# Filters' first transform stage as 32x32 block matmuls, and adaLN sums in pieces, in layer 0's MLP

## The chip, the cores and the metric

The kernel runs on one core of one Trainium2 chip. The metric is the device time of one execution in microseconds (us). The engines of a core work side by side, each through its own list of instructions in order, and wait for each other through semaphores: TensorE (matmuls; PE, its loads of weights PEld), VectorE (DVE), ScalarE (ACT), GpSimd (POOL) and SyncE (SP, which here only issues DMAs).

## What is computed

Two layers over 1024 tokens of width 1024. Layer 0 mixes with a recurrent block (RG-LRU), layer 1 with an order-2 Hyena operator; each is followed by a squared-ReLU MLP of hidden width 4096. Every sub-layer is normed and modulated by sums of the condition vector (adaLN). All data are fp32.

```python
for i in range(DEPTH):
    mod = (cond @ ada_w[i] + ada_b[i])[:, None, :]
    sh1, sc1, g1, sh2, sc2, g2 = jnp.split(mod, 6, axis=-1)
    u = modulate(x, norm_g[i, 0], sh1, sc1)
    ...
    x = x + g1 * y
    x = x + g2 * squared_relu_mlp(modulate(x, norm_g[i, 1], sh2, sc2), mlp_w1[i], mlp_w2[i])

def hyena_filters(L, ...):
    h = jnp.sin(...)                                   # three small layers
    h = (h @ fw4).reshape(L, N_DIRS, HYENA_ORDER, D_MODEL)
    h = h * jnp.exp(-t * deltas)[:, None, None, :]
    h = h / jnp.sum(jnp.abs(h), axis=(0, 1), keepdims=True)
    k = jnp.concatenate([fwd[:1] + bwd[:1], fwd[1:], zeros, jnp.flip(bwd[1:], 0)], axis=0)
    return jnp.fft.rfft(k, axis=0)
```

The filters don't depend on the tokens, so the kernel works them out beside layer 0's MLP, ahead of layer 1, which needs them.

## The kernel before

Activations lie with the 1024 features on 8 tiles of 128 partitions and the 1024 tokens on the columns, in two halves c of 512. A weight tile comes by DMA on SyncE's queue (`raw`, two buffers), ScalarE rounds it to `whi` and VectorE takes the rest, `wlo` (three buffers each), and a product is three matmuls: high by high, high by low, low by high (`mm3`, `gemm`, `gemm2`; lines 133 to 152). Each of these takes one pass through TensorE.

`mlp` goes through eight hidden blocks `fb` of 512. In each, the first matrix gives four hidden tiles for both halves (48 matmuls for a tile and its two halves); `use` squares the rectified values and splits them into `hh` and `hl`. The second matrix then gives the eight output tiles (24 matmuls each for both halves), and `upd` (line 745) adds them to the stream `xs` on VectorE. TensorE's results go to six PSUM banks in turn (`psum`), small sums to a bank of their own (`psum_st`).

From block 1 on, `hook` is called after each hidden tile (4 a block) and each output tile (8 a block), and runs one step of `filters`. There are 64 groups: 16 frequencies g by 4 quarters u. `head(i)` fetches features, lets ScalarE compute the decay into `ht`, multiplies features by weights with three one-pass matmuls, multiplies by the decay on VectorE (line 383) and sums absolute values. `tail(i - 2)` does the first stage of the Fourier transform of a group: one plain fp32 matmul of `ht` by `mf`, a 128x128 matrix with four equal 32x32 blocks on its diagonal; in the trace it is two passes (line 396). ScalarE copies the result to `fe` and a DMA writes it out. The last group of a quarter (g = 0) has another first block, and closes the norm.

`ada_half` computes half of one adaLN vector: eight times a DMA of 128x512 weights (`adaw`, two buffers, line 190) and a multiply-add on VectorE into `acc` (lines 193, 195), then four small fp32 matmuls with ones, eight passes in the trace (line 198), and a short addition. Fourteen halves are left at the MLP of layer 0: two are done inside block 0, then two at the end of each block, with all their instructions issued together.

The order of each engine's list comes from a scheduler that simulates the program; `tc.issue_after(x)` keeps instructions behind x in that order.

Of the kernel before, what the change touches and what calls it, by code (L numbers as in the profile page):

```python
# [16 lines left out]
P = 128  # L17
D = 1024
# [28 lines left out]
def tile_block(ctx: ExitStack, tc: tile.TileContext, a, out, dbg=None):  # L47
# [19 lines left out]
    def psum():  # L67
        return psp.tile([P, 512], F32, tag="ps", name=nm("ps"))
# [116 lines left out]
    def ada_half(pool, l, j, h):  # L185
# [12 lines left out]
            nc.tensor.matmul(ps[:, t:t + 1], acc[:, t * P:(t + 1) * P], ones[:, 0:1], start=True, stop=True)  # L198
        nc.vector.tensor_tensor(mod[:, l, j, 4 * h:4 * h + 4], ps[:, 0:4], vcols("ada_b", 48 * l + 8 * j + 4 * h, 4), op=ALU.add)


    def norm_stats(pool, xs, n, keep, aside=False):

# [82 lines left out]
    def filter_pos(fp, fb, aside):  # L286

        pos = fp.tile([66, 512], F32, tag="pos", name="pos")
        nc.sync.dma_start(pos, a["pos"])
        w1 = fp.tile([66, P], F32, tag="fw1", name="fw1")  # L290
        nc.sync.dma_start(w1, a["fw1"])
        w23 = fp.tile([P, 2, P], F32, tag="fw23", name="fw23")
        nc.sync.dma_start(w23, a["fw23"])
        h = pos
        MAGIC = 12582912.0
        C1 = 6.28125
        C2 = 0.0019350051879882812
        C3 = 2 * math.pi - C1 - C2
        LIM = 3.1415925
        for n in range(3):  # L300
            ps = psum()
            nc.tensor.matmul(ps, w1 if n == 0 else w23[:, n - 1], h, start=True, stop=True)
            s = fp.tile([P, 512], F32, tag="fs", name=nm("fs"), bufs=2)
            nc.vector.tensor_scalar(s, ps, vcol(f"hy_fb{n + 1}", 0), vcol("hy_freq", 0), op0=ALU.add, op1=ALU.mult)
            k = fp.tile([P, 512], F32, tag="fk", name=nm("fk"), bufs=2)
            nc.vector.tensor_scalar(k, s, 1.0 / (2 * math.pi), MAGIC, op0=ALU.mult, op1=ALU.add)
            nc.vector.tensor_scalar(k, k, MAGIC, None, op0=ALU.subtract)
            for cc in (C1, C2, C3):
                nc.vector.scalar_tensor_tensor(s, k, -cc, s, op0=ALU.mult, op1=ALU.add)
            nc.vector.tensor_scalar(s, s, LIM, -LIM, op0=ALU.min, op1=ALU.max)  # L310
            h = fp.tile([P, 512], F32, tag="fh", name=nm("fh"), bufs=2)
            nc.scalar.activation(h, s, AF.Sin)
            aside(n)
        tap("fh3", h)

        lo, up = h[0:64], h[64:128]
        hh = fp.tile([P, 1024], F32, tag="hh", name="hh")
        nc.sync.dma_start(hh[0:64, 512:1024], up)
        nc.sync.dma_start(hh[64:128, 0:511], lo[:, 1:512])
        nc.sync.dma_start(hh[64:128, 1023:1024], lo[:, 0:1])  # L320
        nc.scalar.copy(hh[0:64, 0:512], lo)
        nc.vector.tensor_copy(hh[64:128, 511:1023], up)
        hp = fp.tile([P, 16, 4, 32], F32, tag="hp", name="hp")
        nc.gpsimd.memset(hp, 0.0)
        for half in range(2):
            src = hh[64 * half:64 * half + 64]
            if half:
                src = src[:, ::-1]
            src = src.rearrange("p (t m j g) -> p g m j t", t=16, m=2, j=4, g=8)
            dst = hp.rearrange("p (g m) j t -> p g m j t", m=2)[64 * half:64 * half + 64]  # L330
            for m in range(2):
                for j in range(4):
                    eng = nc.scalar.copy if j % 2 else nc.vector.tensor_copy
                    eng(dst[:, :, m, j, 16 * half:16 * half + 16], src[:, :, m, j, :])
        for n, t in enumerate(split(fb, "hps", hp.rearrange("p g j t -> p (g j t)"), [P, 2048], 1, "v")):
            nc.sync.dma_start(hpd[:, :, n].rearrange("g p c -> p g c"), t.bitcast(F32).rearrange("p (g c) -> p g c", g=16))

# [5 lines left out]

    def filters(fp):

        LAG = 2
        st = {}
        steps = [(u, g) for u in (0, 2, 1, 3) for g in list(range(1, 16)) + [0]]
        mf = fp.tile([P, 2, P], F32, name="mf")
        nc.sync.dma_start(mf, a["mf"])  # L350
        tpos = fp.tile([P, 16], F32, name="tpos")
        nc.sync.dma_start(tpos, a["tpos"])
# [37 lines left out]
                nc.vector.tensor_tensor(acc, acc, ab, op=ALU.add)  # L390

        def tail(i):
            u, g = steps[i]
            o, c = u // 2, u % 2
            p2 = psum()
            nc.tensor.matmul(p2, mf[:, 1 if g == 0 else 0], st.pop(("ht", i)), start=True, stop=True)
            e = fp.tile([P, 512], F32, tag="fe", name=nm("fe"), bufs=2)
            nc.scalar.copy(e, p2)
            if g == 0:

                acc = st["acc", u]
                pc = psum_st()
                for t in range(4):
                    nc.tensor.matmul(pc[:, t:t + 1], acc[:, t * P:(t + 1) * P], ones[:, 0:1], start=True, stop=True)
                nc.vector.reciprocal(rn[:, o, 4 * c:4 * c + 4], pc[:, 0:4])
                pr = psum_rb()
                nc.tensor.matmul(pr, ones, acc, start=True, stop=True)
                sk = fp.tile([17, 512], F32, tag="sk", name=nm("sk"), bufs=1)
                nc.sync.dma_start(sk, a["skip"][:, o, c * 512:(c + 1) * 512])
                nc.vector.tensor_tensor(sk, pr[0:17, :], sk, op=ALU.mult)  # L410
                nc.vector.tensor_tensor(e[0:17, :], e[0:17, :], sk, op=ALU.add)
            b = prow(g)
            nc.sync.dma_start(fd[u][:, b:b + 29:4].rearrange("f k d -> k f d"), e)

        def step(i):
            if i < len(steps):
                head(i)
            if i >= LAG:
                tail(i - LAG)
        return [lambda i=i: step(i) for i in range(len(steps) + LAG)]  # L420

# [283 lines left out]
                use(m, c, pp[c])  # L705


    def mlp(load, l, xs, r0, ada_step, fin=None, normed=lambda: None, hook=lambda: None):

        with ExitStack() as st:  # L710
            uh, ul = [None, None], [None, None]
# [9 lines left out]
            for fb in range(8):  # L721
# [3 lines left out]
                def use(m, c, ps):  # L725
                    r = hp.tile([P, 512], F32, tag="r", name=nm("r"), bufs=2)
                    nc.scalar.activation(r, ps, AF.Relu)
                    h_ = hp.tile([P, 512], F32R, tag="hh", name=nm("hh"), bufs=8)
                    nc.scalar.activation(h_, r, AF.Square)
                    nc.vector.tensor_tensor(r, r, r, op=ALU.mult)  # L730
                    l_ = hp.tile([P, 512], F32R, tag="hl", name=nm("hl"), bufs=8)
                    nc.vector.tensor_tensor(l_, r, h_.bitcast(F32), op=ALU.subtract)
                    hh[c][m], hl[c][m] = h_, l_
                    if c == 1 and fb:
                        hook()

                in_gemm(load, lambda m: a["mlp_w1"][l, 4 * fb + m], 4, uh, ul, use, 3 if fb == 0 else 0)
                if fb == 0:
                    with tc.issue_after(applied[1].ins):
                        ada_step()  # L740
                        ada_step()

                def upd(m, c, ps, o=0, n=512):
                    cs = slice(c * 512 + o, c * 512 + o + n)
                    nc.vector.scalar_tensor_tensor(xs[m][:, cs], ps[:, :n], g2[:, m:m + 1], xs[m][:, cs], op0=ALU.mult, op1=ALU.add)  # L745

                def w2(q, mm, rnd):
                    pp = [psum() for c in rnd]
# [5 lines left out]
                for rnd in ((0,), (1,)) if fb == 7 else ((0, 1),):  # L754
                    for q in range(4):
# [3 lines left out]
                        for mm in range(2):  # L759
                            w2(q, mm, rnd)  # L760
                            if fb and rnd[0] == 0:
                                hook()
                            if fin and fb == 7:
                                fin[0](2 * q + mm, 512 * rnd[0], 512)
                                if rnd == (1,) and q == 0:
# [1 line left out]
                if fin and fb == 7:  # L767
# [8 lines left out]
                    fin[1](768, 256)  # L776
                    fin[2](512, 256)
                    fin[2](768, 256)
                ada_step()
                ada_step()  # L780

    def gemm2_n(pp, w, off, rh, rl, kt):
        if len(pp) == 2:
# [328 lines left out]
    def ada_step(pool):  # L1112
        if ada_todo:
            l, j, h = ada_todo.pop(0)
            ada_half(pool, l, j, h)
            if h == 1 and j == 4:
                make_scale(scl[:, 2 * l + 1], vcols("norm_g", 16 * l + 8, 8), mod[:, l, 4])
            if h == 1 and j == 1:
                make_scale(scl[:, 2], vcols("norm_g", 16, 8), mod[:, 1, 1])

    wst[0], load = open_w()
    wpool = wp_[0]
# [26 lines left out]
        tap("x1", xs[k], k)  # L1149
    with ExitStack() as st:  # L1150
        adap = st.enter_context(tc.tile_pool(name="adap", bufs=1, reuse_waits="tile"))
        ffst, todo = ExitStack(), []

        def normed():

            nst[0].close()
            todo.extend(filters(ffst.enter_context(tc.tile_pool(name="ff", bufs=1, side="right", reuse_waits="tile"))))

        def hook():
            if todo:  # L1160
                todo.pop(0)()
        mlp(load, 0, xs, r0, lambda: ada_step(adap), None, normed, hook)
        assert not ada_todo and not todo
        ffst.close()
    tap("rn", rn)
    open_n()
# [33 lines left out]
def _consts():  # L1200
# [47 lines left out]
    c1_, d1_ = coef(np.arange(32), 1.0), coef(np.arange(16), 2.0)  # L1248
    m1 = np.zeros((2, 16, 8, 4, 32))
    md = np.zeros((2, 4, 32, 16, 8))  # L1250
    mf = np.zeros((2, 4, 32, 4, 32))
    for j in range(4):
        for m in range(2):
            m1[m, :, 4 * m + j, j, :] = c1_[:16]
            md[m, j, :, :, 4 * m + j] = d1_.T
        mf[:, j, :, j, :] = c1_
    mf[1, 0, 16, 0, :] = c1_[0]

    def lay(m, w=P):
        m = m.reshape(-1, P, w).transpose(1, 0, 2)  # L1260
# [9 lines left out]
    pos2 = np.ascontiguousarray(np.concatenate([pos[:512].T, pos[512:].T], 0))  # L1270
    deltas = np.abs(np.linspace(math.log(1e-2) / 1.5, math.log(1e-2) / 0.3, D, dtype=f32))
    full = np.concatenate([t, t[back]], 0)
    tpos = np.ascontiguousarray(full.reshape(32, 2, 4, 8).transpose(3, 1, 2, 0).reshape(16, P).T)
    decay = np.ascontiguousarray(np.broadcast_to(-deltas, (P, D)))
    return dict(m1=lay(m1), md=lay(md), mf=lay(mf), m2=lay(m2[FORD], 192), mi=lay(mi[FORD]), pos=pos2, tpos=tpos, decay=decay)


def _layout(i):
# [81 lines left out]
```

## Time and profile before

| | |
|---|---|
| median of 3 runs | 2838.49 us (2838.48 to 2840.58) |
| profiled execution | 2838.23 us, span 2836.4 us |
| busy: TensorE matmuls | 2682.9 us, 95% |
| busy: loads of weights | 2046.7 us, 72% |
| busy: VectorE | 1524.7 us, 54% |
| busy: ScalarE | 1044.6 us, 37% |
| granted TensorE clock, mean | 0.972 |

Layer 0's MLP lies between about 560 and 1390 us of the span. A matmul's record begins when TensorE takes it up; its end is modelled, so neighbouring matmuls overlap in the record, and the pace is read from starts. `idle before` is time in which the engine stood still just ahead of an instruction, with what ended it.

### The profile page before, as it was taken

The page shows a single profiled execution, that of the slowest core. Times are in us where ns is not written, and L with a number is a line of the kernel's source. Part 1 is how long each engine was busy: PE and PEld are TensorE (multiplying, and loading weights), DVE is VectorE, ACT ScalarE, POOL GpSimd, SP SyncE. Part 2 cuts the span into 40 slices and gives each one's busy share as a digit, 9 for nine tenths or more (in the row PEclk, how much of TensorE's full clock was granted, in tenths as well). Part 3 has the DMA queues.
Part 4 walks back from the last instruction along what each step waited for, and adds up shares of the span by engine and source line. Part 5 has one row for each costly group of instructions (what it writes and reads, how often), then busy time and mean ns, then how long its engine had stood idle before and what let it go on. Part 6 is the DMA issues. An engine that isn't in the chain of part 4 may idle for free. (4 is left out here: it accounts for less than half of the span.)

```text
span 2836.4 us, 29311 instructions
## 1 busy us (share of the span) xinstructions
PE 2682.9 (95%) x11194; PEld 2046.7 (72%) x11194; DVE 1524.7 (54%) x2077; ACT 1044.6 (37%) x1566; POOL 256.7 (9%) x162
## 2 busy tenths in 40 slices
PE   6689898999999999999999999878899999999998
PEld 1577777788777777778888773333588888888887
DVE  7666665875455455443843347647475333333336
ACT  5457577552333333322632223323343211122213
POOL 0223333010000000000100013212000000000000
PEclk8789999999999999999999999999899999999999
DMA  8431123344344344331312325565331111111112
GB/s 302 123 119 45 45 75 104 111 136 138 108 132 138 106 128 138 92 92 47 126 56 93 104 98 154 149 161 167 126 89 45 52 46 52 45 53 45 52 45 97
DMA packets 120269, 286.33 MB, mean 101 GB/s; under 512 B 11770, under 2 KB 27900, under 8 KB 120002
## 3 DMA queue, kind: packets, MB, share of 16 engines
q1 hardware_dynamic: 109618, 261.40, 30.2%
q10 hardware_dynamic: 8256, 14.68, 1.8%
q0 software_dynamic: 2256, 8.39, 0.9%
q8 instruction: 88, 1.44, 0.2%
q14 instruction: 51, 0.42, 0.0%
HBM read 212.86 MB, written 37.75 MB: 88 GB/s over the span
## 5 line engine op out<-in xcount | busy, mean ns | idle before, releaser
L152 PE MATMUL ps<-u,whi 128*128 128x512 f32 x2696 | 734.3, 393 | 0.0
L113 ACT CAST whi<-raw 128x1024 fp32r<-128x1024 f32 x206 | 216.3, 1050 | 1107.6 <-PE ps L152 1012.7
L152 PEld LDWEIGHTS ps<-u,whi 128*128 128x128 f32 x2696 | 504.7, 188 | 113.9 <-issue 7.2
L115 DVE TENSOR_TENSOR wlo<-raw,whi 128x1024 fp32r<-128x1024 f32 x206 | 261.9, 1271 | 473.3 <-ACT whi L113 472.6
L152 PE MATMUL ps<-u,wlo 128*128 128x512 f32 x1348 | 418.5, 390 | 0.1
L152 PE MATMUL ps<-hh,whi 128*128 128x512 f32 x896 | 296.4, 409 | 0.0
L152 PEld LDWEIGHTS ps<-u,wlo 128*128 128x128 f32 x1348 | 252.9, 188 | 53.2 <-DVE wlo L115 0.7
L152 PE MATMUL ps<-hh,wlo 128*128 128x512 f32 x896 | 281.8, 390 | 0.0
L152 PE MATMUL ps<-hl,whi 128*128 128x512 f32 x896 | 280.3, 389 | 0.0
L152 PEld LDWEIGHTS ps<-hh,whi 128*128 128x128 f32 x896 | 168.2, 188 | 51.5 <-issue 17.3
L134 PE MATMUL ps<-u,whi 128*128 128x512 f32 (+1 forms) x508 | 195.3, 386 | 3.5 <-POOL u L260 2.9
L133 PE MATMUL ps<-u,whi 128*128 128x512 f32 (+1 forms) x508 | 187.2, 385 | 11.5 <-ACT u L259 11.5
L135 PE MATMUL ps<-u,wlo 128*128 128x512 f32 (+1 forms) x508 | 193.1, 382 | 1.8 <-DVE wlo L115 1.8
L152 PEld LDWEIGHTS ps<-hl,whi 128*128 128x128 f32 x896 | 168.2, 188 | 36.2 <-issue 1.0
L152 PEld LDWEIGHTS ps<-hh,wlo 128*128 128x128 f32 x896 | 168.1, 188 | 35.1
L745 DVE SCALAR_TENSOR_TENSOR big<-ps,mod,big 128x512 f32<-128x512 f32 (+1 forms) x132 | 91.6, 731 | 185.3 <-PE ps L152 177.7
L745 DVE SCALAR_TENSOR_TENSOR x<-ps,mod,x 128x512 f32<-128x512 f32 x128 | 91.3, 746 | 147.0 <-PE ps L152 139.0
L260 POOL TENSOR_TENSOR u<-nu,u 128x512 fp32r<-128x512 f32 x24 | 33.9, 1413 | 1010.6 <-ACT u L259 1001.4
L195 DVE SCALAR_TENSOR_TENSOR acc<-adaw,cond,acc 128x512 f32<-128x512 f32 x98 | 73.5, 750 | 92.1 <-DMA adaw<-in_ada_w_dram 90.7
L133 PEld LDWEIGHTS ps<-u,whi 128*128 128x128 f32 x508 | 98.0, 194 | 30.1 <-ACT u L259 12.2
L134 PEld LDWEIGHTS ps<-u,whi 128*128 128x128 f32 x508 | 98.2, 193 | 25.5 <-POOL u L260 5.9
L135 PEld LDWEIGHTS ps<-u,wlo 128*128 128x128 f32 x508 | 97.5, 192 | 20.2 <-DVE wlo L115 3.0
(223 smaller groups left out, 3821.3 us busy)
## 6 DMA issues: line engine op xcount, KB each, us to landing
raw<-in_mlp_w_dram SPq DMA_DIRECT2D x136, 512.0 KB
adaw<-in_ada_w_dram SPq DMA_DIRECT2D x112, 256.0 KB
fd<-fe SPq DMA_DIRECT2D x64, 256.0 KB
ft<-fd SPq DMA_DIRECT2D x64, 256.0 KB
e<-big SPq DMA_DIRECT2D x64, 256.0 KB
eraw<-in_ada_w_dram SPq DMA_DIRECT2D x24, 512.0 KB
raw<-in_hy_w_in_dram SPq DMA_DIRECT2D x24, 512.0 KB
big<-e ACTq DMA_DIRECT2D x48, 256.0 KB
```

Of the source, the lines that this page charges most:

```text
L113: lsplit[0] = nc.scalar.copy(hi, raw)
L115: lsplit[1] = nc.vector.tensor_tensor(lo, raw, hi.bitcast(F32), op=ALU.subtract)
L133: first = pin(nc.tensor.matmul(ps, wh, rh, start=start, stop=False))
L134: pin(nc.tensor.matmul(ps, wh, rl, start=False, stop=False))
L135: pin(nc.tensor.matmul(ps, wl, rh, start=False, stop=stop))
L152: nc.tensor.matmul(pp[c], x, y[c][k], start=first, stop=last)
L195: nc.vector.scalar_tensor_tensor(acc, w, s, acc, op0=ALU.mult, op1=ALU.add)
L260: applied[k % 2] = (nc.vector if k % 2 else nc.gpsimd).tensor_tensor(ul[k], u, uh[k].bitcast(F32), op=ALU.subtract)
L745: nc.vector.scalar_tensor_tensor(xs[m][:, cs], ps[:, :n], g2[:, m:m + 1], xs[m][:, cs], op0=ALU.mult, op1=ALU.add)
```

## The change

The transform matrix shrinks from 128x128 to a column of four equal 32x32 blocks. Groups are taken in pairs, an odd and an even frequency: `tail` runs at every second hook, for the groups i - 3 and i - 2, and issues eight plain fp32 matmuls of 32 rows by 32 columns over 512, alternating between the two groups and their two PSUM banks. So that the two groups use different blocks of the array, the rows of odd groups are rotated by 32 where features and decay positions are laid out. The lag grows from 2 to 3, and `ht` from three buffers to four.

Of the adaLN halves, the first two stay. The other twelve are taken apart into eight additions and one closing step each. A hook behind a hidden tile runs two pieces, a hook behind an output tile one; each addition is kept behind the VectorE instruction that ended the hook's MLP work, and the next DMA is issued one piece ahead. Layer 1's calls are unchanged.

```diff
+    def ada_steps(pool, l, j, h):
+        st = {}
+        def fetch(k):
+            st[k] = pool.tile([P, 512], F32, tag="adaw", name=nm("adaw"), bufs=2)
+            c0 = j * D + h * 512
+            nc.sync.dma_start(st[k], a["ada_w"][l, k * P:(k + 1) * P, c0:c0 + 512])
+        def step(k, anchor):
+            if k < NT:
+                if k == 0:
+                    st["acc"] = pool.tile([P, 512], F32, tag="acc", name=nm("acc"), bufs=1)
+                    fetch(0)
+                if k < NT - 1:
+                    fetch(k + 1)
+                w, s, acc = st.pop(k), cond[:, 0, k:k + 1], st["acc"]
+                with tc.issue_after(anchor.ins):
+                    if k == 0:
+                        nc.vector.tensor_scalar(acc, w, s, None, op0=ALU.mult)
+                    else:
+                        nc.vector.scalar_tensor_tensor(acc, w, s, acc, op0=ALU.mult, op1=ALU.add)
+                return
+            ps = psum_st()
+            for t in range(4):
+                nc.tensor.matmul(ps[:, t:t + 1], st["acc"][:, t * P:(t + 1) * P], ones[:, 0:1], start=True, stop=True)
...
-                    eng(dst[:, :, m, j, 16 * half:16 * half + 16], src[:, :, m, j, :])
+                    eng(dst[:, :, m, (j + m) % 4, 16 * half:16 * half + 16], src[:, :, m, j, :])
...
-        LAG = 2
+        LAG = 3
-        mf = fp.tile([P, 2, P], F32, name="mf")
+        mf = fp.tile([P, 2, 32], F32, name="mf")
...
         def tail(i):
+            pp = [psum(), psum()]
+            for j in range(4):
+                for n in range(2):
+                    g = steps[i + n][1]
+                    b = 32 * ((j + g % 2) % 4)
+                    rows = slice(b, b + 32)
+                    nc.tensor.matmul(pp[n][32 * j:32 * j + 32], mf[rows, 1 if g == 0 and j == 0 else 0], st["ht", i + n][rows], start=True, stop=True)
+            for n in range(2):
+                out(i + n, pp[n])
+
+        def out(i, p2):
             u, g = steps[i]
             o, c = u // 2, u % 2
-            p2 = psum()
-            nc.tensor.matmul(p2, mf[:, 1 if g == 0 else 0], st.pop(("ht", i)), start=True, stop=True)
...
-            if i >= LAG:
+            if i >= LAG and i % 2:
                 tail(i - LAG)
...
-                        hook()
+                        hook(ins, 2)
...
-                                hook()
+                                hook(last[0])
...
-                ada_step()
-                ada_step()
...
-        def hook():
+        def hook(anchor, n=1):
             if todo:
                 todo.pop(0)()
+            if not slow:
+                while ada_todo:
+                    slow.extend(ada_steps(adap, *ada_todo.pop(0)))
+            for _ in range(n):
+                if slow:
+                    k, step = slow.pop(0)
+                    step(anchor)
+                    if k == NT:
+                        slow.pop(0)[1](anchor) if slow else None
+                    if slow and slow[0][0] == NT:
+                        break
```

## Rows read from the trace of the kernel before

**Rows 1.** The page, parts 1 and 2: busy time; slices of PE and its granted clock.

```profile
...
PE 2682.9 (95%) x11194; PEld 2046.7 (72%) x11194; DVE 1524.7 (54%) x2077; ACT 1044.6 (37%) x1566; POOL 256.7 (9%) x162
...
PE   6689898999999999999999999878899999999998
...
PEclk8789999999999999999999999999899999999999
...
```

**Rows 2.** Busy time in five stretches, hidden block to hidden block; three and the sum.

```profile
...
core 0: us, PE busy (x) PEld busy (x) DVE busy (x) ACT busy (x) POOL busy (x), PEclk, DMA share, GB/s
715.70:824.20 108.50, 107.91 (x462) 85.07 (x462) 56.50 (x83) 37.02 (x60) 0.00 (x0) 1.00 0.44 126
824.20:934.50 110.30, 109.63 (x471) 86.34 (x470) 58.41 (x86) 37.01 (x60) 0.00 (x0) 1.00 0.42 120
...
1153.80:1262.10 108.30, 107.67 (x460) 84.87 (x459) 50.25 (x72) 35.15 (x57) 0.00 (x0) 1.00 0.34 95
sum 546.40, PE 544.38 PEld 428.96 DVE 280.77 ACT 183.19 POOL 0.00; mean PE 108.88 PEld 85.79 DVE 56.15 ACT 36.64 POOL 0.00
```

**Rows 3.** Waits, 690 to 1270 us (sum, times, longest): all engines, then TensorE.

```profile
...
ACT whi L113 <- PE ps L152: 228.8, 43, 9.6
...
DVE acc L195 <- DMA adaw<-in_ada_w_dram: 67.4, 34, 5.5
...
PE pst L198 <- DVE acc L195: 1.9, 3, 0.7
```

**Rows 4.** Timeline of MLP matmuls: start, length, engine, line, count.

```profile
...
697.42 1.07 PE L152 MATMUL ps<-u,whi 128*128 128x512 f32 x4
...
698.78 0.39 PE L152 MATMUL ps<-u,whi 128*128 128x512 f32 x1
```

**Rows 5.** Timeline at one hook: matmuls, then two loads of weights.

```profile
...
706.04 0.39 PE L135 MATMUL ps<-w,hpg 128*128 128x512 f32 x1
706.27 1.02 PE L396 MATMUL ps<-ht,mf 128*128 128x512 f32 x2
706.73 1.03 PE L152 MATMUL ps<-hh,whi 128*128 128x512 f32 x2
...
706.71 0.19 PEld L152 LDWEIGHTS ps<-hh,whi 128*128 128x128 f32 x1 [0.24 <-issue]
707.13 0.19 PEld L152 LDWEIGHTS ps<-hh,whi 128*128 128x128 f32 x1 [0.24 <-ACT r L727]
...
```

**Rows 6.** Tile ht on TensorE, 718 to 745 us: durations in ns, first, last start.

```profile
...
L396 PE MATMUL ps<-ht,mf x8: 590/590/591, 720.3 to 741.7; 128*128 128x512 f32 x8
...
```

**Rows 7.** Transposes of 2 rows and the matmul behind: timeline, then their line.

```profile
...
24.39 0.40 PE L179 MATMUL ps<-ident,arow 2*128 2x2 f32 x4
...
24.72 0.70 PE L302 MATMUL ps<-fh,fw 128*128 128x512 f32 x1
...
L179 PE MATMUL ps<-ident,arow x16: 195/197/220, 24.4 to 59.3; 2*128 2x2 f32 x16
```

**Rows 8.** The end of one adaLN sum: timeline, then the matmuls' line.

```profile
...
780.24 0.75 DVE L195 SCALAR_TENSOR_TENSOR acc<-adaw,cond,acc 128x512 f32<-128x512 f32 x1 [0.76 <-DMA adaw<-in_ada_w_dram]
...
781.14 1.02 PE L198 MATMUL pst<-ones,acc 128*128 128x1 f32 x8 [0.59 <-DVE acc L195]
...
L198 PE MATMUL pst<-ones,acc x112: 164/250/250, 616.1 to 1220.0; 128*128 128x1 f32 x112
```

**Rows 9.** Groups by line, 690 to 1270 us: busy, mean ns, idle before.

```profile
...
L115 DVE TENSOR_TENSOR wlo<-raw,whi 128x1024 fp32r<-128x1024 f32 x43 | 52.2, 1214 | 0.0
L195 DVE SCALAR_TENSOR_TENSOR acc<-adaw,cond,acc 128x512 f32<-128x512 f32 x64 | 48.1, 751 | 68.4 <-DMA adaw<-in_ada_w_dram 67.4
L383 DVE TENSOR_TENSOR ht<-ps,ht 128x512 f32<-128x512 f32 x62 | 42.4, 683 | 67.7 <-PE ps L135 67.7
...
L398 ACT COPY fe<-ps 128x512 f32<-128x512 f32 x64 | 37.3, 583 | 105.9 <-issue 83.0 <-PE ps L396 23.0
```

**Rows 10.** Waits of SyncE's DMA queue, 540 to 1330 us.

```profile
...
SPq L190 <- DVE acc L195: 63.8, 92, 2.1
...
```

More of the change, by code (lines that the diff above doesn't have):

```diff
@@ L199, in ada_half @@
         nc.vector.tensor_tensor(mod[:, l, j, 4 * h:4 * h + 4], ps[:, 0:4], vcols("ada_b", 48 * l + 8 * j + 4 * h, 4), op=ALU.add)
+    def ada_steps(pool, l, j, h):
[21 more added lines that the diff above has]
+                nc.tensor.matmul(ps[:, t:t + 1], st["acc"][:, t * P:(t + 1) * P], ones[:, 0:1], start=True, stop=True)
+            nc.vector.tensor_tensor(mod[:, l, j, 4 * h:4 * h + 4], ps[:, 0:4], vcols("ada_b", 48 * l + 8 * j + 4 * h, 4), op=ALU.add)
+            ada_done(l, j, h)
+        return [(k, lambda anchor, k=k: step(k, anchor)) for k in range(NT + 1)]
     def norm_stats(pool, xs, n, keep, aside=False):
@@ L705, in in_gemm, with mlp @@
                 use(m, c, pp[c])
-    def mlp(load, l, xs, r0, ada_step, fin=None, normed=lambda: None, hook=lambda: None):
+    def mlp(load, l, xs, r0, ada_step, fin=None, normed=lambda: None, hook=lambda anchor, n=1: None):
         with ExitStack() as st:
@@ L731, in use @@
                     l_ = hp.tile([P, 512], F32R, tag="hl", name=nm("hl"), bufs=8)
-                    nc.vector.tensor_tensor(l_, r, h_.bitcast(F32), op=ALU.subtract)
+                    ins = nc.vector.tensor_tensor(l_, r, h_.bitcast(F32), op=ALU.subtract)
                     hh[c][m], hl[c][m] = h_, l_
                     if c == 1 and fb:
-                        hook()
+                        hook(ins, 2)
                 in_gemm(load, lambda m: a["mlp_w1"][l, 4 * fb + m], 4, uh, ul, use, 3 if fb == 0 else 0)
@@ L741, in mlp @@
                         ada_step()
+                last = [None]
                 def upd(m, c, ps, o=0, n=512):
                     cs = slice(c * 512 + o, c * 512 + o + n)
-                    nc.vector.scalar_tensor_tensor(xs[m][:, cs], ps[:, :n], g2[:, m:m + 1], xs[m][:, cs], op0=ALU.mult, op1=ALU.add)
+                    last[0] = nc.vector.scalar_tensor_tensor(xs[m][:, cs], ps[:, :n], g2[:, m:m + 1], xs[m][:, cs], op0=ALU.mult, op1=ALU.add)
                 def w2(q, mm, rnd):
@@ L1115, in ada_step, with ada_done @@
             ada_half(pool, l, j, h)
[L1116 to L1119, printed above, removed]
+            ada_done(l, j, h)
+    def ada_done(l, j, h):
+        if h == 1 and j == 4:
+            make_scale(scl[:, 2 * l + 1], vcols("norm_g", 16 * l + 8, 8), mod[:, l, 4])
+        if h == 1 and j == 1:
+            make_scale(scl[:, 2], vcols("norm_g", 16, 8), mod[:, 1, 1])
     wst[0], load = open_w()
@@ L1151, in tile_block @@
         adap = st.enter_context(tc.tile_pool(name="adap", bufs=1, reuse_waits="tile"))
-        ffst, todo = ExitStack(), []
+        ffst, todo, slow = ExitStack(), [], []
         def normed():
@@ L1157, in normed @@
             todo.extend(filters(ffst.enter_context(tc.tile_pool(name="ff", bufs=1, side="right", reuse_waits="tile"))))
-        def hook():
+        def hook(anchor, n=1):
             if todo:
                 todo.pop(0)()
+            if not slow:
[9 more added lines that the diff above has]
+                        break
         mlp(load, 0, xs, r0, lambda: ada_step(adap), None, normed, hook)
-        assert not ada_todo and not todo
+        assert not ada_todo and not todo and not slow
         ffst.close()
@@ L1250, in _consts @@
     md = np.zeros((2, 4, 32, 16, 8))
-    mf = np.zeros((2, 4, 32, 4, 32))
     for j in range(4):
@@ L1255, in _consts @@
             md[m, j, :, :, 4 * m + j] = d1_.T
-        mf[:, j, :, j, :] = c1_
-    mf[1, 0, 16, 0, :] = c1_[0]
+    mf2 = np.stack([np.concatenate([c1_] * 4, 0)] * 2, 0)
+    mf2[1, 16] = c1_[0]
     def lay(m, w=P):
@@ L1272, in _consts @@
     full = np.concatenate([t, t[back]], 0)
-    tpos = np.ascontiguousarray(full.reshape(32, 2, 4, 8).transpose(3, 1, 2, 0).reshape(16, P).T)
+    tpos = np.ascontiguousarray(full.reshape(32, 2, 4, 8).transpose(3, 1, 2, 0).reshape(16, 4, 32))
+    tpos[1::2] = np.roll(tpos[1::2], 1, 1)
+    tpos = np.ascontiguousarray(tpos.reshape(16, P).T)
     decay = np.ascontiguousarray(np.broadcast_to(-deltas, (P, D)))
-    return dict(m1=lay(m1), md=lay(md), mf=lay(mf), m2=lay(m2[FORD], 192), mi=lay(mi[FORD]), pos=pos2, tpos=tpos, decay=decay)
+    return dict(m1=lay(m1), md=lay(md), mf=lay(mf2, 32), m2=lay(m2[FORD], 192), mi=lay(mi[FORD]), pos=pos2, tpos=tpos, decay=decay)
 def _layout(i):
```

## The prediction

> **What bounds the kernel now.** I read the share of busy time first: TensorE 95% of the span against VectorE's 54%, and in the slices of layer 0's MLP (the nine from about 640 us on) a full digit at full clock [rows 1]. A share is an average, so next came the same stage cut by its hidden blocks: in five stretches of 546.4 us together TensorE is busy for 544.38, clock 1.00 in each, while VectorE has 281 us of work and ScalarE 183 [rows 2]. Third, the waits of the stage: the long ones are those of ScalarE and VectorE for TensorE, and TensorE's own list has one row, 1.9 us in 3 times, for an adaLN sum [rows 3]. So this stage ends when TensorE has streamed its matmuls. A microsecond taken off TensorE there is one off the kernel, and a microsecond moved on VectorE, ScalarE or a DMA queue is nothing, unless it makes TensorE wait.
>
> **What one group of filters costs on TensorE.** Busy times can't be added (a 0.39 us matmul starts every 0.23 us), so I go by starts. Around one hook the loads of weights show when the array moves on: the weights of a matmul are loaded when the one before it begins to stream. The two passes of the old transform start at 706.27, and the weights of the second MLP matmul behind them are taken at 707.13, so the two passes hold the array for 0.86 us, 0.43 each [rows 5]. The MLP's own matmuls follow each other by 0.227 us, six in 1.36 [rows 4], the last of a group's three feature matmuls is followed after 0.23 [rows 5]. Cross-check: in the second half of a hidden block a hook comes with 24 MLP matmuls, 24 x 0.227 + 3 x 0.23 + 0.86 = 7.0 us, and the transform stands 8 passes in 21.4 us, 4 groups, so 3 periods of 7.0 and the 0.43 to a second pass [rows 6]. All 64 groups, counted by their copies out of PSUM [rows 9]: 64 x 0.86 = 55.0 us of the span are what the first edit works on, 1.72 us a pair of groups.
>
> **Part 1: the transform as 32x32 blocks.** Removed: 2 x 2 passes of 128x128 by 512 columns a pair. Added: eight matmuls of 32 rows and 32 columns by 512, still plain fp32, so by the row of the old one two passes each: 16 loads of weights and 16 passes a pair. The columns that each streams are as many as before. The edit pays only where passes of different blocks stream at the same time. The trace of before has no 32x32 matmul, so the price X of a pair is bounded from rows:
> - Lowest: all eight together as long as one group now, X = 0.86.
> - Issue: if they overlap, but each is taken up in its turn. Four transposes of 2 rows follow each other by 0.067 us, weights and matmul ((0.40 - 0.20) / 3, one being 0.20 long) [rows 7]. Then the last of 16 passes starts at 15 x 0.067 = 1.0 and streams 0.43: X = 1.43. With the pace of full-height loads of 128 columns, 8 in 1.02 us with one 0.25 long, 0.11 each [rows 8], X = 15 x 0.11 + 0.43 = 2.1.
> - Highest: nothing overlaps, 16 x 0.43 = 6.9.
> I take 1.43: blocks of 32 rows are nearer to the row of the 2-row matmuls than to full-height loads, and one row speaks for taking up work ahead: the MLP matmul behind an old transform starts at 706.73 while the second pass, begun about 706.70, still has 0.43 to stream, which the loads confirm [rows 5]. Then 32 x (1.43 - 1.72) = -9.3 us. Ends with overlap: 32 x (0.86 - 1.72) = -27.5 and 32 x (2.1 - 1.72) = +12.
>
> Going from the 2-row matmuls to a full-height one, the first of four and the full one start 0.33 us apart, with no idle time shown between [rows 7]. [...]
>
> Around it, at no cost: 64 copies out of PSUM remain 64 of 0.583 us on ScalarE [rows 9], now two in a row at every second hook. What hides them is 5 to 11 us of MLP matmuls behind each hook. A pair takes two of the six banks at once, beside one of the head and two of the MLP unit; the sixth is the margin. ScalarE is in order and has stood up to 9.6 us at a cast of weights that waits for TensorE [rows 3], so a pair's banks can be held that long; if the cover goes, each pair costs up to one copy, 32 x 0.58 = 19 us. I take 0, since TensorE's list of waits has no bank in it [rows 3]. The lag of 3 instead of 2 and the fourth ht buffer only move the tail later; 67 hooks of the 84 are used. The rotated layout is the same copies and one smaller load, 0.
>
> **Part 2: the adaLN sums in pieces.** The first two halves keep their place. Twelve halves, 2 at the end of a block until now, become 96 pieces at the hooks of blocks 1 to 7, at most 16 a block, with the next load issued a step ahead. VectorE's pieces are the same, 0.75 us each; what goes is its standing for a load, 67.4 us in 34 times [rows 3], which lies beside TensorE's work and is worth nothing by itself. On the path are TensorE's 1.9 us of waits [rows 3]: at 781.14 the sum's matmuls come 0.59 us late, behind the last piece [rows 8]. In pieces the closing matmuls stand one hook after the last addition: -1.9 us, and at worst 0. Behind a piece on VectorE stand the weight split (1.21 us), and the product with the decay (0.68) [rows 9], and the residual additions; TensorE waits for these through three weight buffers, two to three hooks and the banks. Two pieces in a row are 1.5 us against a hook of 12.4 or 7.0. On SyncE's queue a load of a piece now stands between those of weights and features; it has waited there for a sum before too, 63.8 us in 92 times [rows 10], without TensorE paying. Bounds for all this: -1.9 to +3 (two places where TensorE stands out the 1.5 us of two pieces). I take -1.9.
>
> **Sum.** -9.3 - 1.9 = -11.2 us. The profiled execution took 2838.23 us (its span 2836.4 and 1.8 around it, which stay), 0.3 under the median of 2838.49; so 2827.0, by the median 2827.3.
>
> **The rivals.**
> - *Each block stands behind its own first pass* (slower). In the rows matmuls start in the order of the program, and the second pass of a block needs the place and rows of its first. If the queue stops there, block after block takes 0.43 before the next may begin, and only a second pass overlaps the next block's first: X = 8 x 0.43 + 0.43 = 3.87, 32 x (3.87 - 1.72) = +69, 2905. It decides as soon as more than four of the eight stand out a pass (4 x 0.43 = 1.72). For it: the passes of one old matmul start 0.43 apart, never earlier [rows 5, 6]. Against it: the early start at 706.73. [...]
> - *Rows are the shared thing* (no change). Each strip of 32 rows serves two blocks; if one strip feeds one block at a time, it streams 4 passes: X = 4 x 0.43 = 1.72, and only part 2 is left, 2836.6. For it: the change gives neighbours different strips, against it no row.
> - *Nothing overlaps*: X = 6.9, 32 x (6.9 - 1.72) = +166, 3002. It would be the edit not doing what it says.
> - *Another engine becomes the bound*: overlap comes, but banks or VectorE give it back, up to the 19 us above: 2827 + 19 = 2846.
>
> **How the numbers follow.** Overlap with X from 0.86 to 1.55: 0.50. Strips shared, X about 1.55 to 1.9: 0.15. In order behind the first pass: 0.24. Nothing overlaps: 0.05. Gain given back: 0.06. The likeliest is the first, 2827, with its own range 2809 (-27.5 - 1.9) to 2831 (X = 1.55, -5.4 - 1.9). With the strips' case that is 0.65; eight in ten needs the in-order case, so the range goes from 2808 to 2908, the in-order time of 2905 with the 3 us of part 2: 0.50 + 0.15 + 0.24 + 0.06 = 0.95 less what falls past the ends. A measurement can tell about 0.2%, 5.7 us. Faster: 0.50 and a little of the strips' case, 0.51. Same: the rest of it, 0.14. Slower: 0.24 + 0.05 + 0.06 = 0.35.
>
> **What would show it.** The blocks' starts at one hook: 16 starts within 1 us and the next MLP weights 1.4 us after the first one for the forecast; pairs of starts 0.43 apart for the in-order case; loads spaced 0.43 throughout for none. The time between the residual additions of neighbouring blocks (108 to 110 us now [rows 2]) falls by about 2 us or grows by 12. For part 2, TensorE's waits for the sums gone and VectorE's for their loads nearly so, with the end unchanged by it. I am wrong if X lies outside 0.86 to 1.55, or if TensorE's list of waits fills with banks or weight splits.

## The result and the profile after

The changed kernel takes 2821.62 us (median of 6 runs, 2820.28 to 2823.73), the kernel before 2838.48 beside it (6 runs): ratio 0.9944, 95% interval 0.9933 to 0.9955. That is 16.9 us off, where 11.2 were forecast. The profiled execution spans 2820.2 us against 2836.4.

The page of the kernel after, busy time and the slices of TensorE and its granted clock, to be held against [rows 1]:

```profile
...
PE 2667.4 (95%) x11578; PEld 2027.0 (72%) x11578; DVE 1519.5 (54%) x2077; ACT 1044.2 (37%) x1566; POOL 256.7 (9%) x162
...
PE   6789898999999999999999998888899999999998
...
PEclk8789999999999999999999999989899999999999
...
```

Shares and slices hardly differ, and TensorE is busy 15.5 us less with 384 passes more: 64 groups took 128 passes and now take 512. So the gain can't be seen here. The same five stretches between hidden blocks as in [rows 2], cut at the blocks' first residual additions of this kernel (us; busy time and count of each engine; granted clock; DMA share; GB/s):

```profile
...
711.30:815.70 104.40, 104.40 (x532) 80.92 (x531) 55.49 (x83) 37.18 (x60) 0.00 (x0) 1.00 0.44 130
815.70:922.70 107.00, 107.00 (x546) 82.93 (x545) 57.45 (x87) 37.17 (x60) 0.00 (x0) 1.00 0.41 125
...
1135.80:1240.10 104.30, 104.30 (x531) 80.88 (x531) 55.02 (x82) 35.31 (x57) 0.00 (x0) 1.00 0.41 124
sum 528.80, PE 528.80 PEld 409.81 DVE 281.27 ACT 184.01 POOL 0.00; mean PE 105.76 PEld 81.96 DVE 56.25 ACT 36.80 POOL 0.00
```

528.8 us against 546.4, 17.6 less. VectorE's work is the same (281.27 against 280.77) and TensorE is busy all the time, where it lacked 2.0 us. Waits from 690 to 1270 us (sum, times, longest), against [rows 3]:

```profile
...
ACT whi L113 <- PE ps L152: 272.3, 45, 11.2
DVE ht L413 <- PE ps L135: 148.3, 22, 9.4
...
DVE acc L220 <- DMA adaw<-in_ada_w_dram: 0.4, 1, 0.4
...
```

VectorE's 67.4 us of standing for adaLN weights are 0.4. TensorE's own list, one row of 1.9 us before, is empty. The stage is bound by TensorE as before, more cleanly.

The timeline at the first pair of groups (start, length, engine, line, count; then loads of weights), against [rows 5]:

```profile
...
702.58 0.40 PE L135 MATMUL ps<-w,hpg 128*128 128x512 f32 x1
702.90 1.09 PE L430 MATMUL ps<-ht,mf 32*32 32x512 f32 x16
703.92 0.50 PE L152 MATMUL ps<-hh,whi 128*128 128x512 f32 x1
704.25 0.39 PE L152 MATMUL ps<-hl,whi 128*128 128x512 f32 x1
...
702.90 0.18 PEld L430 LDWEIGHTS ps<-ht,mf 32*32 32x32 f32 x16 [0.36 <-ACT whi L113]
703.92 0.19 PEld L152 LDWEIGHTS ps<-hh,whi 128*128 128x128 f32 x1 [0.84 <-ACT r L767]
...
```

All 16 passes of the eight blocks lie within 1.09 us. In the single records eight start between 702.90 and 702.95, some 7 ns apart, and the other eight between 703.36 and 703.40. From the start of the last head matmul to the start of the second matmul behind, 704.25 - 702.58 = 1.67 us pass; two ordinary steps of 0.23 belong to these two, so X = 1.21 us for a pair of groups (38.7 us for the 32 pairs, 1.21 each). Of this 0.86 are two streams of 0.43; the other 0.35 lie at three steps: 0.09 before the first block (0.32 instead of 0.23), 0.16 from the first block to the first full-size matmul behind (1.02 instead of 0.86), most of it at the end of the second batch, and 0.10 at this matmul (0.33 instead of 0.23). The loads show the same places: the first block's weights are taken 0.32 us after the start of the matmul before it, and those of the full-size matmul only at its own start, 703.92, where in [rows 5] weights are loaded while the one before still streams. Old price 1.72, so 32 x (1.21 - 1.72) = -16.3 us, with the sums' -1.9 makes -18.2; the five stretches hold 30 pairs, 30 x 0.51 + 1.9 = 17.2 of the 17.6 found.

Matched instruction by instruction, the changed kernel is about 1 us ahead where the MLP begins, 19.1 at its end, and 16.2 at the end of the program: some 2.9 us come back in the Hyena stage, between about 1700 and 2020 us, which the change doesn't touch. Matched in the same way, the traces of the runs below lie between 4.4 us given back and 2.4 taken off in that stage, and the same kernel run again gives back 1.7. So this differs from execution to execution; its cause stays open.

### The profile page after: what moved, and what is told of

The parts are those of the page before. It is cut to its first block, busy times and chain, and to the rows that moved or that the text cites. A ratio compares the mean times of both kernels' runs of the same rounds, so it can differ in the third digit from the quotient of the medians.

```text
span 2820.2 us, 30100 instructions
## 1 busy us (share of the span) xinstructions
PE 2667.4 (95%) x11578; PEld 2027.0 (72%) x11578; DVE 1519.5 (54%) x2077; ACT 1044.2 (37%) x1566; POOL 256.7 (9%) x162
## 5 line engine op out<-in xcount | busy, mean ns | idle before, releaser
L152 PE MATMUL ps<-hh,wlo 128*128 128x512 f32 x896 | 289.0, 390 | 0.0
L152 PE MATMUL ps<-hl,whi 128*128 128x512 f32 x896 | 287.9, 390 | 0.0
L413 DVE TENSOR_TENSOR ht<-ps,ht 128x512 f32<-128x512 f32 x64 | 43.9, 687 | 163.5 <-PE ps L135 163.5
L133 PEld LDWEIGHTS ps<-u,whi 128*128 128x128 f32 x508 | 97.7, 193 | 30.3 <-ACT u L289 12.3
L135 PEld LDWEIGHTS ps<-u,wlo 128*128 128x128 f32 x508 | 97.4, 192 | 20.7 <-DVE wlo L115 3.6
```

The source lines that it names most:

```text
L133: first = pin(nc.tensor.matmul(ps, wh, rh, start=start, stop=False))
L135: pin(nc.tensor.matmul(ps, wl, rh, start=False, stop=stop))
L152: nc.tensor.matmul(pp[c], x, y[c][k], start=first, stop=last)
L413: nc.vector.tensor_tensor(ht, ps, ht, op=ALU.mult)
```

## Experiments

Each run has its own runs of the kernel before on the same chip: 2836.9 us for part 2 alone, part 1 alone, one group at a visit and the same places, 2837.5 or 2837.6 for the others. The chips differ from that of the result above, so the ratios are the safer comparison. The edits are cut (`...`); they are shown against the changed kernel, that of part 2 alone against the kernel before, and those of the variants of part 1 alone against part 1 alone, the last one against the variant with late closings.

**The change again.** 

> The changed kernel itself, on the chip of the three runs beside it: 0.56% under the kernel before, 2821 where that has 2837.

Measured 2820.43 us, ratio 0.9938 (0.9926 to 0.9951).

**Part 2 alone**: the adaLN sums in pieces, the old transform.

```diff
-                ada_step()
-                ada_step()
...
-                        hook()
+                        hook(ins, 2)
```

> The change without its first part: the old 128x128 transform with lag 2, the adaLN sums in pieces. Theory: only TensorE's three waits go, 1.9 us, 2836.6, which a measurement hardly tells from the kernel before; VectorE no longer stands for the loads. Rival (pieces carry a share): 2828 to 2833. Rival on the other side (pieces delay weight splits): 2840 or more, and a wait of TensorE for a weight split in its list.

Measured 2835.79 us, ratio 0.9994 (0.9985 to 1.0002). TensorE's matmuls have no wait between 690 and 1270 us. The 1.1 us by which it is faster lie within the noise: they fit the 1.9 us that TensorE waited, and don't prove them.

**Part 1 alone**: the 32x32 blocks, the sums again in bursts at the end of a hidden block.

```diff
+                ada_step()
+                ada_step()
...
-            if not slow:
-                while ada_todo:
-                    slow.extend(ada_steps(adap, *ada_todo.pop(0)))
```

> The change without its second part: the transform as 32x32 blocks, the adaLN sums two halves at the end of each hidden block as before. Theory (a pair now holds TensorE 1.22 us by the starts in the trace after, where two old groups held it 1.72; the sums give 1.9): 32 x 0.50 = 16 us under the kernel before, 2822, and TensorE's waits for the sums still there. Rival (the sums in pieces carry a share of the gain, because VectorE's bursts delay the release of banks now that a pair takes two at once): 2826 to 2832, with TensorE waiting at hooks behind a burst.

Measured 2847.67 us, ratio 1.0045 (1.0031 to 1.0058): slower than before, where both theories had it faster. Its waits from 690 to 1270 us, then busy time in three stretches, then VectorE's timeline ahead of one closing matmul:

```profile
...
DVE acc L195 <- DMA adaw<-in_ada_w_dram: 76.6, 40, 7.8
...
PE pst L198 <- DVE acc L195: 17.3, 5, 4.3
...
```

```profile
...
773.30:777.20 3.90, 0.49 (x4) 0.10 (x2) 1.69 (x3) 0.00 (x0) 0.00 (x0) 1.00 0.50 148
777.20:782.20 5.00, 5.00 (x19) 4.14 (x20) 5.00 (x10) 1.15 (x2) 0.00 (x0) 0.66 0.76 216
782.20:800.00 17.80, 17.80 (x90) 13.78 (x89) 9.84 (x16) 5.90 (x10) 0.00 (x0) 1.00 0.61 177
...
```

```profile
...
759.91 0.47 DVE L193 TENSOR_SCALAR acc<-adaw,cond 128x512 f32<-128x512 f32 x1
760.42 0.75 DVE L195 SCALAR_TENSOR_TENSOR acc<-adaw,cond,acc 128x512 f32<-128x512 f32 x1
768.04 1.54 DVE L195 SCALAR_TENSOR_TENSOR acc<-adaw,cond,acc 128x512 f32<-128x512 f32 x2 [6.86 <-DMA adaw<-in_ada_w_dram]
771.67 1.54 DVE L195 SCALAR_TENSOR_TENSOR acc<-adaw,cond,acc 128x512 f32<-128x512 f32 x2 [2.10 <-DMA adaw<-in_ada_w_dram]
775.15 0.75 DVE L195 SCALAR_TENSOR_TENSOR acc<-adaw,cond,acc 128x512 f32<-128x512 f32 x1 [1.94 <-DMA adaw<-in_ada_w_dram]
776.27 0.75 DVE L195 SCALAR_TENSOR_TENSOR acc<-adaw,cond,acc 128x512 f32<-128x512 f32 x1 [0.36 <-DMA adaw<-in_ada_w_dram]
...
```

One half's sum takes 759.9 to 777.0 us, and 11.3 of these 17 are standing for its loads: a chain that the loads pace, not TensorE. In the kernel before TensorE came to the same closing matmul 0.59 us too early [rows 8]; with the shorter transform it comes at 773.8 and stands 3.4 us. Five such waits make 17.3 us. That is what the transform had gained: 30 pairs in the five stretches, 30 x 0.51 = 15.3, and the 1.9 us waited before make 17.2.

Around these waits the granted clock is lower for a while: 0.66 on the mean in the second stretch, and 1.00 again in the third. Where it falls, the pace falls with it: from 778.95 to 781.51 us six full-size matmuls start 0.427 us apart. By hundreds of us from 700 to 1300 the mean clock is 0.98, 0.97, 1.00, 0.97, 0.97 and 0.97, where the kernel before and the changed one have 1.00 in all six. Over the stage 50 full-size matmuls take 0.427 us to the next start instead of 0.227, 10.0 us more, and 29 passes of the closing matmuls 0.213 instead of 0.112, 3.0 us more (the expectations below call it half clock, which the trace of the changed kernel shows from 30 to 40 us as 0.50, and speak of 8 us, from a count of 41 of these matmuls). 17.3 + 10.0 + 3.0 = 30.3. Matched instruction by instruction, this kernel loses 30.4 us on the changed one inside the stage. By the whole execution it is less, 23.9 us between the two profiled ones and 26.1 by the medians: outside the stage, where the two kernels don't differ, this execution was the faster one.

**One group at a visit**: tails of four blocks at every hook instead of eight at every second.

```diff
-            pp = [psum(), psum()]
+            pp = [psum()]
...
-                for n in range(2):
+                for n in range(1):
...
-            if i >= LAG and i % 2:
+            if i >= LAG:
```

> The change with four blocks of one group at every hook instead of eight of two groups at every second. It computes the same. Theory (a visit costs two streams of 0.43 and about 0.36 for going into the small blocks and back, whatever the number of blocks): 1.22 us a group against the 0.86 of the old one, 64 x 0.36 = 23 us over the kernel before less 1.9 for the sums, 2860. Rival (the price is paid block by block, as the forecast's 0.067 us a pass had it): half of a pair's price, 0.61 a group, 2821 as the changed kernel.

Measured 2865.44 us, ratio 1.0098 (1.0085 to 1.0112). The timeline at one visit:

```profile
...
703.03 0.40 PE L135 MATMUL ps<-w,hpg 128*128 128x512 f32 x1
703.35 1.06 PE L430 MATMUL ps<-ht,mf 32*32 32x512 f32 x8
704.34 0.73 PE L152 MATMUL ps<-hh,whi 128*128 128x512 f32 x2
...
```

Eight passes hold the array as long as sixteen did (704.34 - 703.35 = 0.99 us against 1.02). The price is that of a visit, not of a block: 1.18 each, 70 visits (six were split by other matmuls), 82.9 us against 38.7; 44.2 more, and the time is 43.8 above the changed kernel's (45.4, if each is taken against its own kernel before).

**The two groups on the same places**: no rotation, so that blocks j of both groups use one 32x32 place.

```diff
-                    eng(dst[:, :, m, (j + m) % 4, 16 * half:16 * half + 16], src[:, :, m, j, :])
+                    eng(dst[:, :, m, j, 16 * half:16 * half + 16], src[:, :, m, j, :])
...
-                    b = 32 * ((j + g % 2) % 4)
+                    b = 32 * j
```

> The change without the rotation of the odd groups: the blocks of both groups of a pair use the same four places on the diagonal of the array. It computes the same. Theory (blocks overlap where their places differ, and a place serves its own passes one after the other): 4 x 0.43 + 0.36 = 2.08 us a pair, 32 x 0.86 = 27 us over the changed kernel, 2849. Rival (starts are strictly in the order of the program, so a block that has to wait for its place holds up the blocks behind it, in other places too): 8 x 0.43 + 0.43 + 0.36 = 4.2 us a pair, 2917. Rival (the place doesn't matter, small blocks are cheaper by themselves): 2822.

Measured 2848.76 us, ratio 1.004 (1.0026 to 1.0054). The timeline, matmuls and loads of the same visit:

```profile
...
701.82 0.40 PE L135 MATMUL ps<-w,hpg 128*128 128x512 f32 x1
702.14 1.94 PE L430 MATMUL ps<-ht,mf 32*32 32x512 f32 x16
704.01 0.50 PE L152 MATMUL ps<-hh,whi 128*128 128x512 f32 x1
704.35 0.40 PE L152 MATMUL ps<-hl,whi 128*128 128x512 f32 x1
...
702.14 0.17 PEld L430 LDWEIGHTS ps<-ht,mf 32*32 32x32 f32 x8 [0.36 <-ACT whi L113]
702.60 0.14 PEld L430 LDWEIGHTS ps<-ht,mf 32*32 32x32 f32 x4 [0.28 <-issue]
703.03 0.14 PEld L430 LDWEIGHTS ps<-ht,mf 32*32 32x32 f32 x4 [0.28 <-issue]
...
```

X = 704.35 - 701.82 - 0.46 = 2.07: four streams instead of two, and the same 0.35 around them. The 16 passes start in four batches of four, about 0.43 apart. Within the first batch (702.143 to 702.183 in the records) four blocks begin 13 ns apart, twice the 7 ns of the changed kernel, as if every second block of the list were left standing; and the list has both groups' blocks 0, four passes for one place, ahead of the blocks 1. So passes for other places go past those that wait for theirs: each place works off its own. That settles the in-order rival, with the time: 2.07 us a pair, where strict order would have made 4.2.

**Group by group in the program's list**, the rotation kept.

```diff
-            for j in range(4):
-                for n in range(2):
+            for n in range(2):
+                for j in range(4):
```

> The changed kernel with the eight blocks of a pair issued group by group instead of alternating. Theory (every place works off its own passes, the order of the program doesn't matter): as the changed kernel, 2821. Rival (neighbours in one strip of rows hold each other up; the last block of the first group and the first of the second share a strip): one stream of 0.43 more a pair, 14 us more, 2835.

Measured 2822.07 us, ratio 0.9941 (0.9926 to 0.9957): the order in the list doesn't matter when all eight places differ.

**Four groups at a visit**: sixteen blocks on sixteen places at every fourth hook.

```diff
-        LAG = 3
+        LAG = 4
...
-            for n in range(2):
+            for n in range(4):
...
-                    b = 32 * ((j + g % 2) % 4)
+                    b = 32 * ((j + g) % 4)
...
-            if i >= LAG and i % 2:
+            if i >= LAG and i % 4 == 0:
```

> The changed kernel with four groups at every fourth hook: sixteen 32x32 blocks in sixteen places, four rotations of the rows instead of two, lag 4, results copied into the ht buffers instead of fe. It computes the same. Theory (a visit costs two streams and the change of mode, whatever the number of blocks): 0.86 + 0.36 + 0.05 = 1.27 us for four groups instead of 2 x 1.22, 16 x 1.17 = 19 us under the changed kernel, 2802 where the kernel before has 2837. Rival (four of six banks at once make TensorE wait for ScalarE's copies, up to two of 0.58 us a visit): back to 2821, with waits of TensorE behind the copies.

Measured 2830.71 us, ratio 0.9976 (0.9967 to 0.9986): faster than before and 9 slower than the changed kernel. The edit didn't do what it says. In its order other matmuls stand between the blocks, and 16 visits became 45, most of 8, 6 or 24 passes (a likely reason, which no run tests, is that the scheduler places blocks one by one as their four PSUM banks come free); 45 visits at 1.16 us make 52.1 us against 38.7. What sixteen places would give in one piece stays open.

**Part 1 alone, closing matmuls late**: the same bursts, but the sums' closing matmuls put off to the output tiles of the next hidden block, with two buffers for `acc` (and one instead of two for `ab`, for space).

```diff
-        acc = pool.tile([P, 512], F32, tag="acc", name=nm("acc"), bufs=1)
+        acc = pool.tile([P, 512], F32, tag="acc", name=nm("acc"), bufs=2)
...
+                                if mm and late:
+                                    late.pop(0)()
...
-                ada_step()
-                ada_step()
+                late.extend(c for c in (ada_step(), ada_step()) if c)
```

> Blocks as in the change, the adaLN sums of a hidden block in two bursts at its end as before, but their closing matmuls only at the second and fourth output tile of the next hidden block (with a second buffer for the sum, and one instead of two for the absolute values, to make room). It computes the same. Theory (what cost the run without the pieces its gain is TensorE standing at the closing matmuls, 18 us in five waits of 3.6 to 4.7, and the half clock behind each wait, 8 us; not VectorE's bursts as such): the waits go and the gain is there, 2821 to 2825 where the kernel before has 2837. Rival (VectorE's bursts delay the release of banks and weight splits): 2835 to 2847, with TensorE waiting at other lines than the sums'.

Measured 2861.68 us, ratio 1.0085 (1.0071 to 1.0098): slower still, and my theory that only the closing matmuls held TensorE falls. Its waits from 690 to 1270 us:

```profile
...
DVE acc L195 <- DMA adaw<-in_ada_w_dram: 82.3, 40, 8.7
PEld ps L152 <- DVE x L794: 39.4, 15, 4.8
...
PE ps L152 <- DVE x L794: 31.0, 10, 4.5
...
```

The closing matmuls wait no more, but TensorE waits for PSUM banks: VectorE, in order, stands for the sums' loads ahead of the residual additions (L794 here, line 787 of the changed kernel) that empty them. The wait had moved, not gone.

**Part 1 alone, without most of the loads.**

```diff
-            w = pool.tile([P, 512], F32, tag="adaw", name=nm("adaw"), bufs=2)
-            c0 = j * D + h * 512
-            nc.sync.dma_start(w, a["ada_w"][l, k * P:(k + 1) * P, c0:c0 + 512])
+            if k == 0:
+                w = pool.tile([P, 512], F32, tag="adaw", name=nm("adaw"), bufs=2)
+                c0 = j * D + h * 512
+                nc.sync.dma_start(w, a["ada_w"][l, k * P:(k + 1) * P, c0:c0 + 512])
```

> The kernel of e1_blocks_only (32x32 blocks, adaLN sums in bursts as before), but each half's sum loads only the first of its eight weight pieces and uses that one for all eight; so the adaLN values of the later layers are not the layers' own, which is the part of the computation left out. VectorE does the same additions, and stands for an eighth of the loads. Theory (it was VectorE standing for the loads inside the bursts that made TensorE wait in e1, 17.3 us at the closing matmuls and about 8 us of matmuls at half clock after them): the waits go and the time is that of the changed kernel, 2820 to 2824 us. Rival (the bursts' own additions, some 0.6 us each and sixteen in a row, are enough to hold TensorE): as e1_blocks_only, 2843 to 2850 us.

Measured 2818.80 us, ratio 0.9934 (0.992 to 0.9948). VectorE's additions by line, 690 to 1270 us (busy, mean ns, idle before):

```profile
...
L196 DVE SCALAR_TENSOR_TENSOR acc<-adaw,cond,acc 128x512 f32<-128x512 f32 x63 | 47.3, 750 | 1.7
...
```

The additions are there, 63 of 750 ns (not the rival's 0.6 us), in bursts; the standing is 1.7 us, TensorE's list of waits is empty, and the whole gain is back. It was the standing for loads, not the bursts' work. (This run also has fewer transfers; the next one keeps them all.)

**Part 1 alone, closing late, additions on GpSimd**: all loads as before, but GpSimd stands for them.

```diff
-                nc.vector.scalar_tensor_tensor(acc, w, s, acc, op0=ALU.mult, op1=ALU.add)
+                nc.gpsimd.tensor_scalar(w, w, s, None, op0=ALU.mult)
+                nc.gpsimd.tensor_tensor(acc, acc, w, op=ALU.add)
```

> The kernel of e6_late_close (32x32 blocks, bursts, closing matmuls put off), but the additions of the adaLN sums on GpSimd instead of VectorE (a multiplication in place and an addition where VectorE did both in one), all loads as before. Nothing is left out. Theory (in e6 it was VectorE, standing for loads ahead of the residual additions, that kept the PSUM banks from TensorE, 31.0 and 39.4 us of waits): GpSimd stands instead, VectorE is free, the waits for banks go: 2820 to 2826 us. Rival (the loads or the additions cost TensorE by another way, such as the transfers themselves): it stays near e6, 2850 to 2862 us. A third way: GpSimd is so slow at the additions that the closing matmuls wait again, which would show as waits of TensorE for GpSimd's sum.

Measured 2829.19 us, ratio 0.9969 (0.9957 to 0.998): between the two answers. Its waits from 680 to 1270 us, then GpSimd's work by line from 556 to 625, ahead of the stage:

```profile
...
POOL adaw L195 <- DMA adaw<-in_ada_w_dram: 97.4, 49, 6.7
...
PEld ps L152 <- DVE x L795: 7.5, 9, 0.8
...
```

```profile
...
L195 POOL TENSOR_SCALAR adaw<-adaw,cond 128x512 f32<-128x512 f32 x14 | 26.9, 1922 | 6.0 <-DMA adaw<-in_ada_w_dram 5.8
L196 POOL TENSOR_TENSOR acc<-acc,adaw 128x512 f32<-128x512 f32 x14 | 20.7, 1480 | 0.4
L295 POOL TENSOR_TENSOR u<-nu,u 128x512 fp32r<-128x512 f32 x8 | 12.0, 1500 | 2.0 <-ACT u L294 2.0
...
```

Inside the stage the theory holds: GpSimd stands 97.4 us for loads, TensorE's matmuls (PE) have no wait, its loads of weights wait 7.5 us for the residual additions instead of 39.4, and, matched by instructions, from 652 to 1295 us of the kernel before the kernel gains 18.5 us on it (the changed one 19.3). So neither the transfers themselves nor the single buffer for `ab`, both as with the late closings, were what cost TensorE. But it enters the stage 8.6 us late. Between 556 and 625 us GpSimd is busy 60.5 us instead of 10.6, for the first halves' sums are there too, and a part of the norm (L295) that feeds the MLP's first matmuls comes behind them on its list. That loss is outside the question; I read its place from these rows and didn't test it.

## Why the prediction was right, and where it wasn't

- **Overlap or not.** Right, but on thin ground. It was taken at even odds on one row, the MLP matmul that starts early at 706.73 [rows 5]. That row shows work taken up early, not two streams side by side, since the array went on to this matmul's stream only at 707.13. So this step was in part luck.
- **The size of X, the mis-sized term.** Forecast 1.43 with an issue pace of 0.067 us for each of 16 passes; measured 1.21, and -16.3 instead of -9.3 us. Blocks on different places start 7 ns apart, eight within 0.05 us, so issue costs next to nothing; the 2-row transposes [rows 7] weren't the nearest row for that. In its place stands a toll of about 0.35 us for a visit, nearly the same for two streams of four blocks (1.18), two of eight (1.21) and four streams (2.07). Two errors partly cancelled: 1.43 has 0.57 us too much for issue and leaves out 0.35 of toll. That X fell inside 0.86 to 1.55 owes something to that.
- **The toll of changing sizes.** I set it at nothing, since [rows 7] show no idle time at one change. The row says a little more: four steps of 0.067 make 0.27, and the full-size matmul starts 0.33 behind the first, 0.06 later. In the trace after both changes of a pair cost time: 0.09 us on the way in and about 0.24 on the way out, nearly all of the 0.35 by which X, at 1.21, exceeds two streams. What takes this time is not shown by any run here.
- **In order behind the first pass**, 24 in 100, and the cause of the range's high end. It falls with the batches of four: with two blocks to a place, passes for other places start ahead of those that wait for theirs (2.07 us a pair, where strict order would have made 4.2). **Strips of rows shared**: falls too, since eight blocks on four strips start together, within 0.05 us. **Nothing overlaps**: falls. **Banks give it back**: not in the changed kernel, whose TensorE waits for none; the loss by banks did come, in the variant with late closings, by a cause that I hadn't put there.
- **Part 2.** The waits that were to give its -1.9 us are gone, and the time of part 2 alone, -1.1 us, agrees with that, but also with no gain at all. What failed is the step before: "a microsecond taken off TensorE there is one off the kernel". With the sums in bursts the eight-block transform makes the kernel 10.7 us slower, not 16 faster. The 67.4 us of VectorE's standing were not beside TensorE's work with room to spare; they were part of a chain of loads almost as long as TensorE's block. The 1.9 us in [rows 3] and the 0.59 in [rows 8] showed that TensorE was already early by a little, at three places: its slack there was nil. I priced these waits by what they were and not by what they would become once TensorE is 3 us faster per block: 3.2 to 4.3 us each. Since both parts came together, the sum didn't suffer from it.
- **The total**, 5.4 us under the forecast: 7.0 from X, about 1 from before the MLP, less 2.9 in the Hyena stage, of which the last two aren't explained.

## What to carry to other kernels

Ahead of shortening the bound engine's work, look at every place where it waits a little for another: a wait of half a microsecond can mean that the other chain is as long already. Here all that was gained was waited out there, and the lower clock at the five waits of 3.2 to 4.3 us cost another 13.0 us. Loads that an in-order engine stands for belong one piece ahead and between its other work, not in bursts; to move only the consumer moved the wait here to the next thing that this engine serves (31.0 and 39.4 us at the PSUM banks). Small blocks on different places of the array were paid by the visit here (1.18 us for four, 1.21 for eight), so fill the visit (up to eight blocks were measured) and keep its blocks together; with four blocks to a visit the kernel was slower than with the old transform.

## What the runs showed of the hardware

- 32x32 fp32 blocks on eight different places start about 7 ns apart and stream side by side, their second passes 0.46 us behind the first; with two blocks to a place, one goes behind the other (four batches about 0.43 us apart), and blocks for other places pass them (1.21 us for eight blocks on eight places, 2.07 on four).
- A visit to small blocks costs about 0.35 us beside its streams, whether with 8 or 16 passes (1.18 and 1.21 us).
- After standing for 3.4 us TensorE was granted a mean of 0.66 of its clock from 777.2 to 782.2 us, with matmuls 0.43 us apart instead of 0.227 in it, and 1.00 behind: five waits of 17.3 us in all cost another 13.0.
